# Second and fifth sum of the down weights: where their transfers are issued in a hybrid diffusion layer

## The chip, the core and the metric

The kernel runs on one core of a Trainium2 chip. A core has TensorE (matmul; the profile calls it PE, and its weight loads PEld), VectorE (DVE), ScalarE (ACT), GpSimd (POOL) and SyncE (SP). Each engine works through its own queue in order, and waits at an instruction until the semaphores it names are there. Transfers (DMA) are issued from the queues of SP, POOL and, once, ACT; sixteen DMA engines carry them out. The metric is the time of the slowest core in device microseconds; with one core that is this core's time.

## The reference

One layer on 512 latent tokens of width 1024, with 256 context tokens: a modulated norm, one input projection that feeds a bidirectional Mamba-2 branch and a windowed attention, their merge, and a gated ConvFFN. Cut to what matters here:

```python
p_lat = h_lat @ w_in                                   # z, x/B/C, dt, q, k, v, gates
y_l, _, _ = ssd_bidir(xs_l, bm_l, cm_l, dt_l, la_l, hf_c, hb_c, True)    # the branch
ssd_lat = ssd_output(y_l, xs_l, z, d_skip, ssd_g)
att_lat = window_ctx_attention(q_l, k_l, v_l, k_c, v_c, sink)
x = x + gt1 * ((g_ssd * (ssd_lat @ w_o_ssd) + g_att * (att_lat @ w_o_att)) @ w_out)

def conv_ffn(h, w_up, conv_w, conv_b, w_down):
    u = dwconv_centred(h @ w_up, conv_w, conv_b)       # 2 * 2816 channels
    a, b = u[..., :D_FF], u[..., D_FF:]
    return (jax.nn.silu(a) * b) @ w_down               # the down product, 2816 to 1024

x = rmsnorm(x + gt2 * conv_ffn(modulate(x, norm2_g, sh2, sc2), ...), final_g)
```

The shifts, scales and gates (sh, sc, gt) come from silu(c) @ w_mod.

## The kernel before

Every wide product is made of three passes in a reduced float format: a weight of 128x1024 is loaded by SP (`wraw`, three buffers), ScalarE casts it to a high part (`whi`, L223), VectorE subtracts that to get the low part (`wlo`, L224; L1166 and L1169 in the attention), and TensorE multiplies high by high, high by low and low by high (L295 to L298).

In order of time the program has these stages: the first projections with the modulation (0 to about 60 us), the attention with the q, k, z and output weights beside it (to about 380), the branch (about 430 to 720), the merge and the output projection (to about 860), 22 up steps of the ConvFFN (to 1098), and the down product (to the end).

**The sums of weights.** The down product is made by seven products of half size in place of eight. Four of the operands are sums of the weight's quarters `wdn[0]` to `wdn[3]`, whose signs are folded in by the host. They are computed by transfers alone, in DRAM: a copy of one addend into the sum, then an accumulating transfer of the other. `added` makes the pair; the second waits for the first. With the tile names of the profile: dsum1 = wdn2 + wdn3, dsum4 = wdn0 + wdn2, the second sum dsum2 = dsum4 + wdn3, and the fifth dsum5 = dsum2 + wdn1. Each is cut into four slices of 704 KB, so each sum has four copies and four adds. For eight of the up steps there are sums of the same kind (usum). All of these are issued on POOL's queue by `sum_step` (L182 to L190).

**What sets their order.** `in_turn` mixes the lists of pairs: it keeps three (or four) runs alive and takes one transfer of each in turn. In the attention `product_atoms` (L1143) walks through the weights beside it, numbered g; behind the low part of each, `low` issues the next one to four transfers (L1168), and each waits for that subtraction. The fifth sum goes through the list `LATE`, behind the low parts of the up weights of steps 18 to 21 (`behind`, L232), two for each step.

**The branch** runs over four groups of eight heads. In each, `ssd_steps` goes through four chunks of tokens: POOL scales the states (`st`), makes the diagonals and sums y, VectorE weighs x (`xw`) and adds the states, TensorE multiplies (L1659, L1816, L1824). At the end of a group `gate` (L1857) puts the group's rows to DRAM on SP's queue. Next to the group's end stand the last `ssq` of POOL and, behind it, the first state product of the next group. The next group's projection weights (`wx`), the modulation weights (`wm`, used by VectorE at L868 and L870), decays (`fb`, `far`) and z rows come in on SP's queue around that place.

**The modulation's fold.** A quarter of the modulation is summed over the 128 partitions by nine transfers on POOL's queue, each waiting for the one before: `fold` (L846 to L850), fold6 early in the up steps and fold7 in the late ones. `folded(7)` on VectorE (L854) reads the result before the down product; behind it, in `row_tiles`, a small transpose on TensorE (L2434) stands at the head of the down product.

Of the kernel before, what the change touches and what calls it, by code (L numbers as in the profile page):

```python
# [13 lines left out]
ALU = mybir.AluOpType  # L14
# [10 lines left out]
NFF = 22  # L25
# [14 lines left out]
def raw(ap):  # L40
    return ap.bitcast(F32)
# [3 lines left out]
def tile_hybrid_layer(  # L45
# [33 lines left out]
    V, S, G, T = nc.vector, nc.scalar, nc.gpsimd, nc.tensor  # L79
# [68 lines left out]
            src["dn", DU * j + u] = t[:, 1024 * u : 1024 * u + n], n  # L148

    US = dpool.tile([P, 4, len(SEVEN) * 512], F32, name="usum")  # L150
    SUMS, LATE = [], []

    def added(o, x, y):
        return [(o, x, {}), (o, y, dict(accum_op=ALU.add, max_dma_last_dim=DK * P))]

    def in_turn(runs, n):
        out, live = [], []
        runs = list(runs)
        while runs or live:
            while runs and len(live) < n:  # L160
                live.append(list(runs.pop(0)))
            for r in live:
                out.append(r.pop(0))
            live = [r for r in live if r]
        return out

    RUNS = []
    for q in range(4):
        c = slice(q * DK * P, (q + 1) * DK * P)
        two, four = DSUMS[2][:, c], DSUMS[4][:, c]  # L170
        RUNS.append(added(four, wdn[0][:, c], wdn[2][:, c]) + added(two, four, wdn[3][:, c]))
        RUNS.append(added(DSUMS[1][:, c], wdn[2][:, c], wdn[3][:, c]))
        LATE.append(added(DSUMS[5][:, c], two, wdn[1][:, c]))
    for i in range(0, len(SEVEN), 2):
        c = slice(512 * i, 512 * min(i + 2, len(SEVEN)))
        a0, a1, b0, b1 = (wup7[:, u, c] for u in range(4))
        one, two, three, four = (US[:, u, c] for u in range(4))
        RUNS.append(added(one, b0, b1) + added(two, one, a0) + added(four, two, a1))
        RUNS.append(added(three, a0, b0))
    SUMS, LATE = in_turn(RUNS, 3), in_turn(LATE, 4)  # L180
    BEHIND = mybir.DependencyInfo(mybir.DependencyClass.Sync, mybir.DependencyReason.DATA)

    QUEUED = mybir.DependencyInfo(mybir.DependencyClass.NoSync, mybir.DependencyReason.SCHED_ONLY)
# [1 line left out]
    def sum_step(ins, n=1, SUMS=SUMS):  # L185

        for _ in range(min(n, len(SUMS))):
            o, x, how = SUMS.pop(0)
            dma = G.dma_start(o, x, **how)  # L189
            tc.add_manual_dep(dma.ins, ins.ins.name, BEHIND, reason="weight sums behind a split")  # L190
# [41 lines left out]
    def behind(key):  # L232
        if key[0] == "up":
            SPLITS[key[1]] = F["cast"], F["sub"]
            if key[1] % NFF > 17:
                sum_step(F["sub"], 1, LATE)

    def pinned(t, casts=(), lows=()):
# [246 lines left out]
    with tc.tile_pool(name="spool", bufs=1) as sp:  # L485
# [235 lines left out]
        r = {}  # L721
        cq = tmp("te")[:, :LC]
        for j in range(KT):
# [46 lines left out]
            x = ("hi", "lo") if j >= NU else ("hh", "hl")  # L770
# [31 lines left out]
        for n in range(2):  # L802
            for j in range(KT):
                x = ("hi", "lo") if j >= NU else ("hh", "hl")
# [338 lines left out]
    def product_atoms(g, key, accs):  # L1143

        kind, t = key
        d, R, G_ = {}, 1e6 + 100 * g, "%d" % g
# [19 lines left out]
            S.copy(d["w"][0], d["r"])  # L1166

        def low():  # L1168
            sum_step(V.tensor_tensor(d["w"][1], d["r"], raw(d["w"][0]), ALU.subtract), 1 + (g > 3) + (g > 13) + (g > 21))  # L1169

        def rope_part(f):
            scale = -0.125 if kind == "k" else 1.0
# [37 lines left out]
        rw = R - 2e6 if g != 1 else -500  # L1210
        atom("w" + G_, "ACT", 1.05, was, rw, high, late=g > OLD)
        atom("v" + G_, "DVE", 1.225, ["w" + G_], rw, low, late=g > OLD)
        ks = range(-4 if kind == "k" else 0, 8)
        for k in ks:
# [426 lines left out]
    def ssd_steps(g):  # L1641
        d = GR[g]
# [214 lines left out]
        def gate():  # L1857
            for ct in range(4):
                yz = d["zt"][:, ct, :]
                nc.sync.dma_start(yz_d[4 * g + ct], yz)  # L1860
                SQUARES.append(yz)

        r = [([], states)]
        for c in range(4):
# [895 lines left out]
```

## Time and profile before

| | |
|---|---|
| median of 3 runs | 1213.29 us (1212.75 to 1218.32) |
| profiled execution | 1212.78 us, span of its instructions 1210.8 us |
| TensorE busy | 1198.6 us of the span, 99%, granted clock 0.999 |
| VectorE, ScalarE, GpSimd busy | 946.7, 709.3, 313.3 us |
| transfers | 247.41 MB, 204 GB/s; POOL's queue 44.05 MB, 16.5% of the engines' time |
| sum transfers | 32 on dsum (704 KB), 32 on usum (512 KB) |
| their issue on POOL | dsum from 92.0 us to 1092.6 us, usum from 227.2 to 343.2 us |

How to read it: a busy TensorE includes the modelled ends of its pipelined matmuls, so that a gap of a few tenths of a microsecond can hide. Rows of a timeline give the start, the duration, the engine, the line, output and inputs by name, and in brackets the idle time before with what ended it; "issue" is a wait that the profile does not explain. Issue rows of transfers give the median time from issue to landing; the duration of an issue on POOL is that of making the descriptors, not of the transfer.

### The profile page before, as it was taken

Reading aid. Unit: us, or ns where it says so; the run is one execution under the profiler, and the core shown is the slowest. Engines: PE = TensorE matmul, PEld = TensorE weight load, DVE = VectorE, ACT = ScalarE, POOL = GpSimd, SP = SyncE. Lnnn points to the kernel's source line nnn. Section 1 sums busy time; section 2 is a strip of 40 time slices with the busy share of each in tenths; the row PEclk is TensorE's granted clock in tenths of the full one; section 3 lists DMA queues with packets and bytes.
Section 4 is the critical chain, followed back from the end, with each engine's and each line's share of the span. In section 5 each row is a group of like instructions: output and inputs, shape, how many; then the busy total and the mean of one; then the engine's idle time right before and its main releaser. Section 6 shows DMA issues by size and latency. Waiting matters only on the chain.

```text
span 1210.8 us, 18602 instructions
## 1 busy us (share of the span) xinstructions
PE 1198.6 (99%) x6717; PEld 1014.4 (84%) x6717; DVE 946.7 (78%) x1489; ACT 709.3 (59%) x1311; POOL 313.3 (26%) x314
## 2 busy tenths in 40 slices
PE   9999999999999999999999999999999999999998
PEld 6798888888878878788788778888989998887886
DVE  5857887888666588698887877777699998867787
ACT  5557887787543557486575664223547664345654
POOL 0001112222302647265383681000201211030021
PEclk9999999999999999999999999999999999999999
DMA  9656789998977737566577768677467655579662
GB/s 366 262 144 176 170 232 263 237 210 220 247 192 248 222 116 189 178 152 161 173 173 236 211 203 275 217 255 236 129 163 201 177 179 178 174 204 305 218 186 96
DMA packets 144652, 247.41 MB, mean 204 GB/s; under 512 B 28232, under 2 KB 79728, under 8 KB 144560
## 3 DMA queue, kind: packets, MB, share of 16 engines
q1 hardware_dynamic: 119728, 201.91, 53.8%
q0 software_dynamic: 24544, 44.05, 16.5%
q8 instruction: 53, 0.87, 0.3%
q14 instruction: 39, 0.32, 0.1%
q10 hardware_dynamic: 288, 0.27, 0.1%
HBM read 219.24 MB, written 61.80 MB: 232 GB/s over the span
## 4 chain that ended last, share of the span: by engine, by line
PE 82%; issue 10%; DMA 3%; DVE 2%; POOL 1%; ACT 1%; SPq 0%; DVEq 0%; POOLq 0%; ACTq 0%
PE acc L295 13%; PE acc L298 13%; PE acc L296 13%; PE score L1036 3%; PE po L1085 3%; PE pt L1072 3%; PE mis L639 2%; PE mis L1816 2%; PE mis L1659 2%; DMA xs_d<-xb 2%; PE mis L1824 1%; PE mis L2598 1%; PE acc L2597 1%; PE acc L2598 1%; PE acc L2596 1%
## 5 line engine op out<-in xcount | busy, mean ns | idle before, releaser
L295 PE MATMUL acc<-hlh,whi 128*128 128x512 f32 x472 | 192.8, 409 | 0.0
L298 PE MATMUL acc<-hlh,wlo 128*128 128x512 f32 x472 | 185.5, 393 | 0.0
L296 PE MATMUL acc<-hll,whi 128*128 128x512 f32 x472 | 185.0, 392 | 0.0
L223 ACT CAST whi<-wraw 128x1024 fp32r<-128x1024 f32 (+1 forms) x99 | 103.3, 1044 | 133.1 <-PE acc L296 82.0
L224 DVE TENSOR_TENSOR wlo<-wraw,whi 128x1024 fp32r<-128x1024 f32 (+1 forms) x99 | 129.0, 1304 | 53.6 <-ACT whi L223 52.2
L298 PEld LDWEIGHTS acc<-hlh,wlo 128*128 128x128 f32 x472 | 88.6, 188 | 19.9 <-issue 0.5
L295 PEld LDWEIGHTS acc<-hlh,whi 128*128 128x128 f32 x472 | 88.8, 188 | 17.6 <-issue 2.8
L296 PEld LDWEIGHTS acc<-hll,whi 128*128 128x128 f32 x472 | 88.9, 188 | 17.4 <-issue 2.2
L295 PE MATMUL acc<-mh,whi 128*128 128x512 f32 x240 | 93.5, 390 | 0.0
L296 PE MATMUL acc<-ml,whi 128*128 128x512 f32 x240 | 93.4, 389 | 0.0
L298 PE MATMUL acc<-mh,wlo 128*128 128x512 f32 x240 | 93.4, 389 | 0.0
L1045 DVE CUSTOM_DVE_ANT_0 p<-score,winm,nsink 128x512 f32<-128x512 f32 (+1 forms) x64 | 51.8, 810 | 15.8 <-PE score L1036 14.3
L189 POOL DMA_DIRECT2D dsum<-wdn x24 | 25.1, 1153 | 140.0 <-DVE wlo L1169 82.1
L870 DVE SCALAR_TENSOR_TENSOR tm<-wraw,csil,tm 128x512 f32<-128x512 f32 x56 | 45.7, 816 | 16.7 <-DMA wraw<-wm 16.0
L1052 ACT ACTIVATE p<-p,mneg 128x512 f32<-128x512 f32 (+1 forms) x64 | 49.7, 777 | 15.4 <-DVE mneg L1045 14.8
L1080 DVE TENSOR_TENSOR ptl<-pt,pth 128x512 fp32r<-128x512 f32 x72 | 47.5, 685 | 9.7 <-ACT pth L1076 8.2
L295 PE MATMUL acc<-hch,whi 128*128 128x256 f32 x176 | 53.2, 302 | 0.0
L298 PEld LDWEIGHTS acc<-mh,wlo 128*128 128x128 f32 x240 | 45.1, 188 | 9.4
L295 PEld LDWEIGHTS acc<-mh,whi 128*128 128x128 f32 x240 | 45.1, 188 | 9.3
L296 PEld LDWEIGHTS acc<-ml,whi 128*128 128x128 f32 x240 | 45.1, 188 | 9.1
L1169 DVE TENSOR_TENSOR wlo<-wraw,whi 128x1024 fp32r<-128x1024 f32 x30 | 36.7, 1222 | 18.3 <-ACT whi L1166 18.2
L1781 ACT ACTIVATE E<-fb,TX 128x128 f32<-128x128 f32 x128 | 44.6, 390 | 9.9 <-DMA fb<-cs_d 6.1
(553 smaller groups left out, 3528.6 us busy)
## 6 DMA issues: line engine op xcount, KB each, us to landing
wraw<-wup SPq DMA_DIRECT2D x36, 512.0 KB, 4.1
dsum<-wdn POOLq DMA_DIRECT2D x24, 704.0 KB, 9.4
wraw<-wm SPq DMA_DIRECT2D x32, 512.0 KB, 4.4
fb<-cs_d SPq DMA_DIRECT2D x32, 512.0 KB, 8.1
usum<-wup POOLq DMA_DIRECT2D x24, 512.0 KB, 8.9
wraw<-wx SPq DMA_DIRECT2D x24, 512.0 KB, 3.9
wm<-wm SPq DMA_DIRECT2D x16, 512.0 KB, 8.2
wraw<-wz SPq DMA_DIRECT2D x16, 512.0 KB, 6.7
```

What stands on the lines that cost most here:

```text
L223: F["cast"] = S.copy(hi[:, :n], r[:, :n])
L224: F["sub"] = V.tensor_tensor(lo[:, :n], r[:, :n], raw(hi[:, :n]), ALU.subtract)
L295: T.matmul(ps, wh, xh[:, k0 + k, :], start=a, stop=False)
L296: T.matmul(ps, wh, xl[:, k0 + k, :], start=False, stop=False)
L298: T.matmul(ps, wl, xh[:, k0 + k, :], start=False, stop=b)
L870: V.scalar_tensor_tensor(acc, r[:, u * 512 : u * 512 + 512], sc, acc, ALU.mult, ALU.add)
L1036: T.matmul(ps[:, o : o + len(z) * P], Q[h][:, b * P : (b + 1) * P], k[:, j, z[0] * P : (z[-1] + 1) * P], start=v == 0 and o % 512 in (0, P ...
L1045: V.tensor_tensor_reduce(p[:, :w], d["ps"][i][:, o0 : o0 + w], m, op0=ALU.add, op1=ALU.min, scale=1.0, scalar=nsink[:, h : h + 1], accum_o ...
L1052: S.activation(p, p, AF.Exp, bias=d["mneg"][:, i : i + 1], scale=-1.0, accum_out=d["den"][:, i : i + 1])
L1080: V.tensor_tensor(d["ptl"][x], d["pt"][x], raw(d["pth"][x]), ALU.subtract)
L1169: sum_step(V.tensor_tensor(d["w"][1], d["r"], raw(d["w"][0]), ALU.subtract), 1 + (g > 3) + (g > 13) + (g > 21))
L1781: e0 = S.activation(E[:, u, :], F4[:, u, :], AF.Identity, bias=TX[:, c, 0, h : h + 1])
```

## The change

The transfers that make the second sum (dsum2) leave the list of the attention and go into a list of their own, `MID`: four copies, then four adds. `gate` issues up to three of them behind each group of heads, on POOL's queue, in program order: three copies behind the first group, a copy and two adds behind the second, two adds behind the third. They wait for no subtraction. In the attention the count behind a weight is now one, two from g = 4 and three from g = 20 (before: one, two from 4, three from 14, four from 22), for 48 transfers in place of 56. The fifth sum starts at step 16 in place of 18, so its eight transfers go behind the subtractions of steps 16 to 19.

```diff
-    RUNS = []
+    RUNS, MID = [], []
...
         two, four = DSUMS[2][:, c], DSUMS[4][:, c]
-        RUNS.append(added(four, wdn[0][:, c], wdn[2][:, c]) + added(two, four, wdn[3][:, c]))
+        RUNS.append(added(four, wdn[0][:, c], wdn[2][:, c]))
+        MID.append(added(two, four, wdn[3][:, c]))
...
-    SUMS, LATE = in_turn(RUNS, 3), in_turn(LATE, 4)
+    SUMS, MID, LATE = in_turn(RUNS, 3), in_turn(MID, 4), in_turn(LATE, 4)
...
-            if key[1] % NFF > 17:
+            if key[1] % NFF > 15:
                 sum_step(F["sub"], 1, LATE)
...
-            sum_step(V.tensor_tensor(d["w"][1], d["r"], raw(d["w"][0]), ALU.subtract), 1 + (g > 3) + (g > 13) + (g > 21))
+            sum_step(V.tensor_tensor(d["w"][1], d["r"], raw(d["w"][0]), ALU.subtract), 1 + (g > 3) + (g > 19))
...
                 nc.sync.dma_start(yz_d[4 * g + ct], yz)
                 SQUARES.append(yz)
+            for _ in range(min(3, len(MID))):
+                o, x, how = MID.pop(0)
+                tc.keep_in_program_order(G.dma_start(o, x, **how))
```

The rows of the order below name tiles with their numbers; lines of the changed kernel stand one to four higher than those of the kernel before. PE, DVE, ACT and SP have the same rows in the same order in both.

POOL at the end of the second group of heads (ssq is the last of the group, st the first state product of the next). Before:

```order
L1636 TENSOR_TENSOR zs_5562<-y_5989,zs_5562 128x4x128
L1636 TENSOR_TENSOR y_6150<-te_6132,te_6139 128x512
L1633 TENSOR_TENSOR ssq_115<-ssq_115,sq_6209 128x512
L1636 TENSOR_TENSOR st_6342<-st_6309,eT_3695 128x512
L1636 TENSOR_TENSOR st_6355<-st_6342,eT_3695 128x512
```

Now:

```order
L1637 TENSOR_TENSOR zs_5557<-y_5984,zs_5557 128x4x128
L1637 TENSOR_TENSOR y_6145<-te_6127,te_6134 128x512
L1634 TENSOR_TENSOR ssq_115<-ssq_115,sq_6204 128x512
L1865 DMA dsum2_76<-dsum4_77 128x1408
L1865 DMA dsum2_76<-wdn 128x4x352 x2
L1637 TENSOR_TENSOR st_6340<-st_6307,eT_3687 128x512
L1637 TENSOR_TENSOR st_6353<-st_6340,eT_3687 128x512
```

A copy and two adds now stand between the last ssq of the group and the first state product of the next.

POOL in the late up steps, from the third transfer of the fold on (fold7 is the modulation's fold, mod2 its result). Before:

```order
L848 DMA fold7_767<-fold7_767 128x128
L189 DMA dsum5_78<-dsum2_76 128x1408
L848 DMA fold7_767<-fold7_767 64x128
L848 DMA fold7_767<-fold7_767 32x128
L189 DMA dsum5_78<-dsum2_76 128x1408
L848 DMA fold7_767<-fold7_767 16x128
L848 DMA fold7_767<-fold7_767 16x64
L189 DMA dsum5_78<-dsum2_76 128x1408
L848 DMA fold7_767<-fold7_767 16x32
L850 DMA mod2_95<-fold7_767 128x4x1
L189 DMA dsum5_78<-dsum2_76 128x1408
L189 DMA dsum5_78<-wdn 128x4x352 x4
```

Now:

```order
L190 DMA dsum5_78<-dsum2_76 128x1408
L849 DMA fold7_767<-fold7_767 128x128
L190 DMA dsum5_78<-wdn 128x4x352
L849 DMA fold7_767<-fold7_767 64x128
L849 DMA fold7_767<-fold7_767 32x128
L190 DMA dsum5_78<-wdn 128x4x352
L849 DMA fold7_767<-fold7_767 16x128
L849 DMA fold7_767<-fold7_767 16x64
L190 DMA dsum5_78<-wdn 128x4x352
L849 DMA fold7_767<-fold7_767 16x32
L851 DMA mod2_95<-fold7_767 128x4x1
L190 DMA dsum5_78<-wdn 128x4x352
```

The first three copies of dsum5 have moved ahead of the fold's first transfer (not shown here); where copies stood between its links there are adds now, and one add is left behind its end, where a copy and four adds were.

More of the change, by code (lines that the diff above doesn't have):

```diff
@@ L150, in tile_hybrid_layer @@
     US = dpool.tile([P, 4, len(SEVEN) * 512], F32, name="usum")
-    SUMS, LATE = [], []
+    LATE = []
     def added(o, x, y):
```

## The prediction

> **What bounds the kernel now.** I read the head of the page first, then busy time by stretches, then the places where TensorE is short of its full time.
>
> ```profile
> span 1210.8 us, 18602 instructions
> PE 1198.6 (99%) x6717; PEld 1014.4 (84%) x6717; DVE 946.7 (78%) x1489; ACT 709.3 (59%) x1311; POOL 313.3 (26%) x314
> ```
>
> TensorE is idle for 1210.8 - 1198.6 = 12.2 us. No arithmetic is changed, so only these idle microseconds can be won, and any time is lost only where a transfer or a queue makes TensorE wait. The stretches (start:end in us, length, then busy time and count of PE, PEld, DVE, ACT, POOL, the granted clock, the DMA share, GB/s) say where they lie:
>
> ```profile
> 60.00:380.00 320.00, 318.53 (x1730) 273.06 (x1729) 240.51 (x476) 223.39 (x426) 52.19 (x57) 1.00 0.82 212
> 430.00:660.00 230.00, 229.49 (x1400) 189.41 (x1399) 194.23 (x293) 148.16 (x350) 121.26 (x109) 1.00 0.62 169
> 660.00:720.00 60.00, 58.81 (x328) 46.77 (x327) 48.60 (x69) 37.46 (x86) 42.86 (x38) 1.00 0.69 202
> 1010.00:1100.00 90.00, 90.00 (x399) 74.43 (x399) 72.31 (x102) 39.08 (x52) 17.48 (x18) 1.00 0.67 189
> 1100.00:1115.00 15.00, 13.70 (x60) 10.74 (x59) 11.08 (x15) 8.10 (x10) 0.00 (x0) 1.00 1.06 339
> 1170.00:1211.00 41.00, 34.96 (x163) 29.14 (x161) 34.70 (x51) 22.20 (x35) 5.18 (x7) 0.96 0.42 135
> ```
>
> Idle time of TensorE: 1.47 us in the attention (60 to 380), 0.51 + 1.19 us in the branch (430 to 720), none in the last up steps, 1.30 us at the start of the down product, and 41.00 - 34.96 = 6.0 us (5.8 of them within the span) at the end, which the change does not touch. So at most about 1.47 + 0.51 + 1.19 + 1.30 = 4.5 us is to be won, less than the 0.5% (6.1 us) that a measurement of this kernel can tell from no change.
>
> The 1.30 us at the start of the down product have one cause. First the chain of waits, then TensorE's own rows:
>
> ```profile
> 1099.05 1.24 DVE wlo L224
> 1100.30 8.51 DMA wraw<-wdn
> 1108.84 1.05 ACT whi L223
> 1109.92 1.24 DVE wlo L224
> ...
> 1109.94 0.50 PE L2596 MATMUL mis<-whi,fs 128*128 128x512 f32 x1 [0.77 <-ACT whi L223]
> 1111.20 0.50 PE L2598 MATMUL mis<-wlo,fs 128*128 128x512 f32 x1 [0.53 <-DVE wlo L224]
> ```
>
> A weight load that takes 8.51 us is what the split, and TensorE, wait for. Transfers by issue (out<-in, queue, count, KB, median us to landing), the whole run first, then the three single issues at 1100.3 (weight), 1081.0 (copy) and 1081.6 (add):
>
> ```profile
> dsum<-wdn POOLq DMA_DIRECT2D x24, 704.0 KB, 9.4
> wraw<-wdn SPq DMA_DIRECT2D x11, 512.0 KB, 3.6
> ...
> wraw<-wdn SPq DMA_DIRECT2D x1, 512.0 KB, 8.5
> dsum<-dsum POOLq DMA_DIRECT2D x1, 704.0 KB, 4.4
> dsum<-wdn POOLq DMA_DIRECT2D x1, 704.0 KB, 10.6
> ```
>
> The load needs 3.6 us as a rule and 8.5 us here, where the fifth sum's four adds are in flight: 4.9 us more is the price of adds beside a load.
>
> **The change part by part.** It removes and adds no instruction on TensorE, VectorE or ScalarE; it moves eight transfers (704 KB each, four copies and four adds) from the attention to the branch, and the fifth sum's eight by two up steps.
>
> *Down start.* Rows of GpSimd's queue before it (start, us, what, count, idle time before), with the consumer of the modulation fold on VectorE and on TensorE:
>
> ```profile
> 1057.57 0.81 POOL L189 DMA_DIRECT2D dsum<-dsum  x1
> 1061.25 0.79 POOL L848 DMA_DIRECT2D fold<-fold  x1 [2.87 <-DMA fold<-fold]
> 1080.21 0.84 POOL L850 DMA_DIRECT2D mod<-fold  x1 [3.66 <-DMA fold<-fold]
> 1081.59 3.98 POOL L189 DMA_DIRECT2D dsum<-wdn  x3
> 1092.60 1.25 POOL L189 DMA_DIRECT2D dsum<-wdn  x1 [7.03 <-DVE fs L2123]
> ...
> 1096.41 0.15 DVE L854 TENSOR_TENSOR mod<-mod,vec 128x4 f32<-128x4 f32 x1
> 1098.00 0.27 PE L2434 MATMUL mis<-ident,g2c 128*8 128x128 f32 x1
> ```
>
> Four adds left here from 1081.59 to 1092.60. Now three leave before the fold's end and one behind it, at about 1092, so that only one is still in flight when the load leaves at 1100.30. TensorE reaches its weight at 1109.94 - 0.77 = 1109.2, so the load has 1109.2 - 1100.30 - 1.05 - 1.24 = 6.6 us, against 3.6 us alone. I take the whole 1.30 us as won; the ends are 0 (the remaining add holds it back as before) and -1.3.
>
> *The fold in GpSimd's queue.* The late modulation fold (fold7) is a chain of nine transfers, each of which waits for the one before it. Before, three copies stand between its links; now one copy and three adds do. The queue keeps its order: the link at 1061.25 took 4.3 us behind the copy of 1057.57, the next, with nothing ahead of it, 2.1 us.
>
> ```profile
> fold<-fold POOLq DMA_DIRECT2D x1, 32.0 KB, 4.3
> fold<-fold POOLq DMA_DIRECT2D x1, 16.0 KB, 2.1
> ```
>
> I let a link behind an add land 1.4 us after it, an estimate: two thirds of the 2.1 us that one takes alone. With 9.4 us for an add: first add at 1057.8, its link lands at 1068.6; next link 1071; add at 1069.4 lands 1078.8, links 1080.2 and 1083.2; add at 1081 lands 1090.4, link 1091.8; the last one is issued at 1092 and lands at 1095. VectorE asks for it at 1096.41 (before, it was issued at 1080.21): nothing is lost, by 1.4 us. With the 10.6 us of the crowded add the chain ends three times 1.2 us later, at 1098.6; then VectorE adds, negates, and TensorE transposes at about 1099.2 in place of 1098.00: +1.2 us. I take 0; ends 0 and +1.2.
>
> *The branch.* GpSimd issues three transfers behind the first group of heads, three behind the second, two behind the third. It sits idle there:
>
> ```profile
> 503.50 1.06 POOL L1636 TENSOR_TENSOR st<-st,eT 128x512 f32<-128x512 f32 x1 [14.64 <-ACT st L1680]
> 582.15 1.06 POOL L1636 TENSOR_TENSOR st<-st,eT 128x512 f32<-128x512 f32 x1 [8.30 <-ACT st L1680]
> 660.28 1.06 POOL L1636 TENSOR_TENSOR st<-st,eT 128x512 f32<-128x512 f32 x1 [8.34 <-ACT st L1680]
> ```
>
> At the issue cost in these rows (1.3 us for an add, from 3.98 us for three, and under 0.8 for a copy) three need at most 3.4 of 8.3 us, and every sum that they wait for landed long before, in the attention or a group earlier. Queued behind them is the state product (st), which waits for ScalarE anyway. So the issue costs nothing. The transfers themselves do not: they fly beside the loads of the next group. The one that is used as soon as it lands is the modulation weight, and VectorE stands still for it, with the state weights (xw) for TensorE queued behind. The loads left at 580.5 and 656.4:
>
> ```profile
> wraw<-wm SPq DMA_DIRECT2D x1, 512.0 KB, 4.8
> wraw<-wm SPq DMA_DIRECT2D x1, 512.0 KB, 6.0
> ...
> 588.18 0.75 DVE L1478 SCALAR_TENSOR_TENSOR ta<-acc,half,ta 128x511 f32<-128x511 f32 x1 [0.83 <-ACT ta L1477]
> 589.44 0.68 DVE L1647 TENSOR_TENSOR xw<-xs,TD 128x512 f32<-128x512 f32 x1
> 590.66 1.02 PE L1659 MATMUL mis<-xw,Bk 128*128 128x512 f32 x2
> ...
> 662.39 1.54 DVE L870 SCALAR_TENSOR_TENSOR tm<-wraw,csil,tm 128x512 f32<-128x512 f32 x2 [2.08 <-DMA wraw<-wm]
> 663.85 1.29 DVE L1647 TENSOR_TENSOR xw<-xs,TD 128x512 f32<-128x512 f32 x2
> 665.30 1.02 PE L1659 MATMUL mis<-xw,Bk 128*128 128x512 f32 x2
> ```
>
> Behind the second group VectorE has 0.83 us of idle time and TensorE 590.66 - 590.12 = 0.54 us of slack: lateness beyond 1.4 us is paid. Behind the third the first of two xw ends at about 664.5, so lateness beyond 0.8 us is paid. If each load takes 8.5 us (the row at 1100.3), it is 3.7 and 2.5 us late, and costs 2.3 + 1.7 = 4.0 us. If the adds put their 4.9 us on top of what the loads take now, it is 3.5 + 4.1 = 7.6 us. If the adds have mostly passed by then (they leave from 582.15 - 8.30 = 573.9 and 660.28 - 8.34 = 651.9 on, the loads 4 to 7 us later), it is 0. I take half of the 4.0, +2.0, since adds of 9.4 us end just after the loads would. The three copies behind the first group leave from 503.50 - 14.64 = 488.9 on and have landed by about 500; the state product that follows needs none of them: 0.
>
> The Trainium skill (DMA: Bandwidth & Descriptors, "Anatomy of one DMA — SWDGE (gpsimd) path") fits a transfer from this queue with 2.0 us plus its bytes at 436 GB/s, which makes an estimated 3.7 us for 704 KB; the adds' rows here (9.4 and 10.6 us) say otherwise, and only the copy's 4.4 us comes near. By the page the adds would be gone before either load leaves and the branch would cost 0 in place of +2.0.
>
> *Attention.* Two transfers go beside each weight in the middle where three went, and eight fewer in all. Its 1.47 us of idle time are nearly all one wait:
>
> ```profile
> 208.60 0.36 PE L1036 MATMUL score<-khi,q 128*128 128x256 f32 x1 [1.42 <-DVE wlo L1169]
> ```
>
> Two sum transfers stand beside the weights there before and after, so I take -0.3; ends -1.5 (gone) and 0.
>
> *Up steps.* The adds now fly at 1058 to 1090 beside the up weights, where TensorE has no idle time. A weight's buffer is one of three, and each weight lasts TensorE about 5.4 us, so a load has some 11 us before its split; 4.9 us more is covered: 0.
>
> Sum: -1.3 (down) + 0 (fold) + 2.0 (branch) - 0.3 (attention) + 0 = **+0.4 us** on the profiled execution's 1212.78 us, so 1213.2; the median of the runs shown stands 0.5 us above that execution: **1213.7 us**.
>
> **The rivals.**
> - *The branch hides its transfers.* GpSimd's idle 8.3 us and a DMA share of 0.62 speak for it, the 2.08 us for which VectorE already waits on a modulation weight against it. Then -1.3 - 0.3 = -1.6: 1211.7.
> - *The adds crowd the group boundaries*, the slower side: each modulation load pays the full 4.9 us, VectorE stands, and TensorE pays 7.6 us, less the 1.3 and 0.3: +6.0, so 1219.3. For it speaks the 8.5 us load; against it that at 1100 adds had queued on one another for 18 us, while here only two leave together. It decides from about 0.8 to 1.4 us of lateness of the load.
> - *The fold comes late.* Its slack is only 1.4 us by my sum; +1.2 on top of the forecast: 1214.9. If the adds took 12 us each, it would be three times 2.6 - 1.4 - 1.2 = 5.2 us, but no add alone in its queue does.
> - *The waits in all stages go* (attention, branch and down), the most the idle rows allow: -4.5, 1208.8.
>
> **How the numbers follow.** Forecast 0.50 (1212 to 1216), hidden branch 0.27, crowded boundaries 0.11, late fold 0.08, all waits gone 0.04. Range 1209.5 to 1218.5: it takes in the hidden branch and late fold and leaves out most of the two ends. Faster by over 0.5% is beyond all idle time that can be won, so 0.04; slower by over 0.5% (above 1219.4) is half of the crowded case with a little for a mechanism that I don't see, 0.07; within 0.5%: 0.89.
>
> **What would show it.** Down start: the load that left at 1100.3 lands in under 6.6 us and the stretch 1100 to 1115 has no idle TensorE. Fold: its last transfer is issued between 1085 and 1094, and VectorE has no wait before the add at L854 (L855 after). Branch: longer waits for wraw<-wm behind groups two and three, and gaps of TensorE before L1659 of 0 to 4 us in sum. Wrong would be idle time of GpSimd's issue on the path of st, a TensorE gap in the up steps, or a sum that is not there when the down steps load it.

## The result, and the profile after

The changed kernel takes 1229.01 us (median of 4 runs, 1224.12 to 1229.56) against 1213.02 us of the kernel before beside it (median of 4, 1212.14 to 1218.32). The ratio is 1.0114, with a 95% interval of 1.0075 to 1.0152: **slower by about 1.1%**, where 1213.7 us and no measurable change were forecast. The profiled execution took 1229.16 us.

The head of the page after:

```profile
span 1227.3 us, 18605 instructions
...
PE 1202.4 (98%) x6717; PEld 1016.6 (83%) x6717; DVE 944.5 (77%) x1489; ACT 708.4 (58%) x1311; POOL 313.5 (26%) x314
```

The span is 16.5 us longer. TensorE is idle for 24.9 us in place of 12.2, and busy for 3.8 us more with the same 6717 instructions. The stretches after that answer to those shown of before (the last one, the start of the down product, stands 16.4 us later now):

```profile
60.00:380.00 320.00, 319.94 (x1738) 274.62 (x1737) 239.73 (x475) 224.04 (x427) 46.07 (x51) 1.00 0.74 195
430.00:660.00 230.00, 221.72 (x1360) 183.56 (x1359) 185.65 (x281) 143.34 (x341) 125.36 (x115) 0.99 0.64 176
660.00:720.00 60.00, 55.04 (x280) 42.04 (x279) 43.30 (x62) 31.00 (x73) 32.50 (x30) 0.94 0.82 228
1010.00:1100.00 90.00, 88.58 (x415) 73.71 (x414) 72.47 (x99) 38.50 (x55) 17.08 (x17) 1.00 0.68 201
1116.40:1131.40 15.00, 15.00 (x69) 12.41 (x68) 12.86 (x17) 10.32 (x13) 0.00 (x0) 1.00 0.85 285
```

The attention has won its 1.4 us and the down start its 1.3 us; in the branch (430 to 720) TensorE is busy for 11.5 us less of the same 290 us, and the granted clock is below 1.00.

TensorE runs the same instructions in the same order in both kernels, so the start of one and the same instruction can be compared. How many microseconds later it starts than in the profile of before, at points of the program named by their time in that profile (a row of each later experiment is put here too, so that the reader can come back to it; in e3, e7, e8, e12 and e13 a few neighbouring rows of TensorE are swapped, which moves the figures by tenths at most):

```
start in before      205   215   428   436   500   512   586   594   660   680   708   716   850   862  1000  1060  1105  1115
the change           0.0  -1.7  -2.1  -1.3  -1.3   0.4   0.4   8.8   8.8  16.5  16.5  15.1  15.3  16.3  16.3  18.3  18.3  16.4
e4_held (same)       0.4  -1.2  -1.7  -1.4  -1.4   0.2   0.1   8.9   8.9  14.7  14.7  13.3  13.5  15.7  15.7  15.7  15.7  13.9
e2_branch_alone     -0.3  -2.0  -2.4  -2.1  -2.1  -0.9  -0.9   8.7   8.7  16.7  16.7  15.3  15.6  16.7  16.7  16.7  16.7  14.9
e1_late_alone       -0.3  -0.1  -0.2   0.4   0.4   0.4   0.4   0.4   0.4   0.4   0.4  -1.0  -0.8   0.5   0.5   0.5   0.5  -1.3
e3_first_chunk      -0.2  -1.9  -2.3  -1.9  -1.5  -1.5  -0.4  -0.4   1.5   1.5   1.5   0.1   0.3   1.9   1.9   1.9   1.9   0.0
e5_plain             0.2  -1.5  -1.8  -1.3  -1.3   0.0   0.0   3.5   3.5   8.1   8.1   7.9   8.2  10.1  10.1  10.1  10.1   8.3
e7_held_order        0.0  -1.6  -1.6  -1.3  -1.3  -1.3   0.2   0.2   1.8   6.1   6.3   9.1   8.5   9.1   9.1   9.1   9.1   7.3
e8_held_before       0.0   2.0   2.1   2.5   2.5   2.5   3.9   3.9   5.5   5.5   5.8   6.9   6.6   7.4   7.4   7.4   7.4   5.5
e9_one_by_one       -0.1  -1.7  -2.1  -1.5  -1.5  -1.6   0.1   0.1   1.7   5.5   5.5   8.6   8.0   8.5   8.5   8.5   8.5   6.7
e10_mid_in_up       -0.2  -1.9  -1.9  -1.4  -1.4  -1.4  -1.4  -1.4  -1.4  -1.4  -1.4  -1.1  -1.7  -1.2  -1.1   2.2   2.2   0.4
e11_before_again     0.5   2.6   2.5   3.2   3.2   3.2   3.2   3.2   3.2   3.2   3.2   1.8   2.2   5.4   5.4   5.4   5.4   4.4
e12_away_from_wm    -0.1  -1.8  -2.2  -1.7  -1.2  -1.2  -1.3  -1.3  -1.3  -1.3  -1.3  -1.6  -2.2   2.1   2.1   2.1   2.1   0.3
e13_one_copy_moved  -0.3  -2.0  -2.4  -1.7  -1.1  -1.1  -1.1  -1.1  -1.1  -1.1  -1.1  -1.0  -1.5  -1.3  -1.3  -1.3  -1.3  -2.8
```

The loss is made at three places in the main: behind the first group of heads (500 to 512, +1.7), behind the second (586 to 594, +8.4) and behind the third (660 to 680, +7.7). Smaller losses stand at 850 to 862 (+1.0) and in the up steps at 1000 to 1060 (+2.0); the second of these is missing in the other profile of the same instructions (e4_held). What stands at the three places is VectorE waiting for modulation weights. The waits by pair (who, for whom, total, times, longest), first of before, then of after:

```profile
DVE tm L870 <- DMA wraw<-wm: 16.0, 11, 3.3
```

```profile
DVE tm L871 <- DMA wraw<-wm: 36.7, 11, 9.0
```

The single issues of that load behind groups 1, 2 and 3, of the projection weight just ahead of the second one in SP's queue, and of the transfers that the change puts there (three copies; two adds behind group 2; two adds behind group 3), after:

```profile
wraw<-wm SPq DMA_DIRECT2D x1, 512.0 KB, 6.8
...
wraw<-wm SPq DMA_DIRECT2D x1, 512.0 KB, 13.6
...
wraw<-wm SPq DMA_DIRECT2D x1, 512.0 KB, 11.5
...
wraw<-wx SPq DMA_DIRECT2D x1, 512.0 KB, 12.3
...
dsum<-dsum POOLq DMA_DIRECT2D x3, 704.0 KB, 11.6
...
dsum<-wdn POOLq DMA_DIRECT2D x2, 704.0 KB, 15.6
...
dsum<-wdn POOLq DMA_DIRECT2D x2, 704.0 KB, 15.3
```

The prediction's rows have 4.8 and 6.0 us for the second and third load; they are now 8.8 and 5.5 us longer. The projection weight at 578.2 took 5.7 us before and 12.3 now. Behind group 2 the lateness grows along SP's queue: 6.6 us for this weight, 7.7 for the store issued behind it (`ts_d<-tb`, 4.4 us before, 12.1 now), 8.8 for the modulation weight behind both. All sixteen DMA engines are full there. The queues in the stretch 580 to 592 (packets, MB, share of the sixteen engines' time; q1 is SP's queue, q0 GpSimd's), first of before, where GpSimd's has nothing, then of after:

```profile
q1 hardware_dynamic: 731, 2.10, 49.0%
...
q0 software_dynamic: 945, 1.30, 62.0%
q1 hardware_dynamic: 963, 2.05, 50.3%
```

Together the two queues ask for 112% of the engines' time; the stage's mean of 0.64 (0.62 before) hides this. Whether the full engines alone make the lateness, or the turns between the two queues add to it, was not taken apart. The rows of TensorE behind group 1, and of VectorE and TensorE behind groups 2 and 3, with the idle time ahead of each:

```profile
508.80 1.12 PE L1660 MATMUL mis<-xw,Bk 128*128 128x512 f32 x2 [1.47 <-DVE xw L1648]
```

```profile
594.56 0.75 DVE L871 SCALAR_TENSOR_TENSOR tm<-wraw,csil,tm 128x512 f32<-128x512 f32 x1 [9.05 <-DMA wraw<-wm]
...
677.01 1.54 DVE L871 SCALAR_TENSOR_TENSOR tm<-wraw,csil,tm 128x512 f32<-128x512 f32 x2 [7.91 <-DMA wraw<-wm]
678.47 0.68 DVE L1648 TENSOR_TENSOR xw<-xs,TD 128x512 f32<-128x512 f32 x1
```

```profile
596.06 2.04 PE L1660 MATMUL mis<-xw,Bk 128*128 128x512 f32 x2 [6.77 <-DVE xw L1648]
...
679.21 2.08 PE L1660 MATMUL mis<-xw,Bk 128*128 128x512 f32 x2 [4.96 <-DVE xw L1648]
```

The two products mis<-xw,Bk took 1.02 us before (the prediction's rows at 590.66 and 665.30) and take 2.04 and 2.08 here. The clock that was granted in and behind the gap, in stretches of 3 us (the last three columns are the granted clock, the DMA share and GB/s):

```profile
588.00:591.00 3.00, 1.28 (x8) 0.83 (x6) 0.00 (x0) 0.53 (x1) 0.00 (x0) 1.00 1.09 292
591.00:594.00 3.00, 0.00 (x0) 0.00 (x0) 0.00 (x0) 0.00 (x0) 0.00 (x0) 0.71 1.04 287
594.00:597.00 3.00, 0.94 (x1) 0.50 (x2) 2.44 (x4) 0.00 (x0) 0.00 (x0) 0.50 0.00 0
597.00:600.00 3.00, 3.00 (x14) 2.20 (x12) 2.71 (x6) 0.63 (x1) 1.44 (x1) 0.65 0.50 175
600.00:603.00 3.00, 3.00 (x19) 2.54 (x18) 3.00 (x7) 1.50 (x3) 1.44 (x1) 1.00 0.02 5
```

So a gap of 6.8 us is followed by some 3 us of work at half speed. That makes the cost at group 2 (8.4 us) larger than the gap. Half-speed work behind this gap and the one behind group 3 is what can make up the 3.8 us by which TensorE is "busier".

### The profile page after: what moved, and what is told of

The parts are those of the page before. It is cut to its first block, busy times and chain, and to the rows that moved or that the text cites. A ratio compares the mean times of both kernels' runs of the same rounds, so it can differ in the third digit from the quotient of the medians.

```text
span 1227.3 us, 18605 instructions
## 1 busy us (share of the span) xinstructions
PE 1202.4 (98%) x6717; PEld 1016.6 (83%) x6717; DVE 944.5 (77%) x1489; ACT 708.4 (58%) x1311; POOL 313.5 (26%) x314
## 3 DMA queue, kind: packets, MB, share of 16 engines
q0 software_dynamic: 24544, 44.05, 16.5%
## 4 chain that ended last, share of the span: by engine, by line
PE 76%; issue 11%; DMA 6%; DVE 4%; POOL 1%; ACT 1%; SPq 0%; DVEq 0%; POOLq 0%; ACTq 0%
PE acc L299 12%; PE acc L296 12%; PE acc L297 11%; DMA wraw<-wm 3%; PE score L1037 3%; PE po L1086 3%; PE pt L1073 2%; PE mis L640 2%; PE mis L1817 2%; PE mis L1660 2%; PE mis L2600 2%; PE mis L2602 2%; PE mis L2601 2%; PE mis L1825 1%; PE acc L2600 1%
## 5 line engine op out<-in xcount | busy, mean ns | idle before, releaser
L296 PEld LDWEIGHTS acc<-hlh,whi 128*128 128x128 f32 x472 | 89.1, 189 | 17.8 <-issue 2.9
L190 POOL DMA_DIRECT2D dsum<-wdn x20 | 20.7, 1086 | 128.9 <-DVE wlo L1170 125.9
L1488 ACT ACTIVATE tb<-ta 128x512 f32<-128x512 f32 (+1 forms) x44 | 23.4, 534 | 50.8 <-DVE ta L1482 50.8
```

The source lines that it names most:

```text
L296: T.matmul(ps, wh, xh[:, k0 + k, :], start=a, stop=False)
```

## The experiments

Theory A: transfers of GpSimd's queue beside a group boundary hold back SP's queue; the modulation load at its end is late; VectorE stands for it with xw behind, and TensorE for xw. Rivals: the fifth sum's place carries the loss (D); any such transfers cost that much wherever they stand (B); only the accumulating ones do (C); the projection weights of the same queue would stop TensorE anyway (E).

### The two parts apart

```diff
 e1_late_alone: the change, but
-        RUNS.append(added(four, wdn[0][:, c], wdn[2][:, c]))
-        MID.append(added(two, four, wdn[3][:, c]))
+        RUNS.append(added(four, wdn[0][:, c], wdn[2][:, c]) + added(two, four, wdn[3][:, c]))
...
-            sum_step(V.tensor_tensor(...), 1 + (g > 3) + (g > 19))
+            sum_step(V.tensor_tensor(...), 1 + (g > 3) + (g > 13) + (g > 21))
 e2_branch_alone: the change, but
-            if key[1] % NFF > 15:
+            if key[1] % NFF > 17:
```

> The second sum is back in the attention as before; only the fifth sum stands beside steps 16 to 19. Theory A (the loss of the change is made at the group boundaries of the branch, where the added transfers hold up the modulation weight that VectorE stands for): the branch and the attention are as before; the down start wins about 1.7 us and the up steps lose about 2.0 us, so +0.3 us on 1213.0, ratio 1.000 within 0.002. Rival D (the fifth sum beside steps 16 to 19 carries a good part of the loss): at least +5 us, 1218 or more.

> Only the second sum moves to the gates of the branch; the fifth sum is beside steps 18 to 21 as before. Theory A: attention -1.7, boundaries +1.6, +8.4 and +7.6, -1.4 at the wait near 710 us, +1.0 at the modulation load near 859 us: +15.5 us, so about 1228.5 us, ratio 1.012 to 1.014, with the same three gaps of TensorE before the products mis<-xw,Bk and the 1.3 us stall at the start of the down product as before. Rival D (the fifth sum's place): 1215 or less.

e1_late_alone: 1211.18 us, ratio 0.9993 (0.9980 to 1.0006). e2_branch_alone: 1231.72 us, ratio 1.0154 (1.0132 to 1.0176). The whole loss is in the branch part; D falls. The profiled execution of e2 is the fastest of its five (1227.57 us), so the table shows 4 us less of e2 than its median. The second and third gap stand where they stood:

```profile
595.15 2.05 PE L1660 MATMUL mis<-xw,Bk 128*128 128x512 f32 x2 [7.16 <-DVE xw L1648]
...
678.98 2.07 PE L1660 MATMUL mis<-xw,Bk 128*128 128x512 f32 x2 [4.83 <-DVE xw L1648]
```

Two things went another way than expected. e1 shows no loss in the up steps (0.5 at 862 and at 1105), and e2 has no stall at the start of the down product (16.7 to 14.9), though the fifth sum is in its old place there. Both come back below.

### The same transfers, another place

```diff
 e3_first_chunk: the change, but the loop over MID goes from gate() to the end of chunk_in(c)
+            if not c:
+                for _ in range(min(3, len(MID))):
+                    o, x, how = MID.pop(0)
+                    tc.keep_in_program_order(G.dma_start(o, x, **how))
```

> The change with the same eight transfers of the second sum, three, three and two, on the same queue, but issued in the first chunk of groups 0, 1 and 2 (about 435, 515 and 595 us), where the transfer engines are at 0.2 to 0.4, and not behind the groups. Theory A: the modulation loads at the boundaries take 4 to 6 us again and the gaps before mis<-xw,Bk go; left are attention -1.7, up +2.0, down -1.7: 1210.5 to 1214 us. Rival B (eight such transfers beside the branch cost some 2 us each wherever they stand, by issue on POOL's queue or by bandwidth): 1225 to 1229 us.

1212.49 us, ratio 0.9999 (0.9986 to 1.0012). The three modulation loads at the boundaries take what they took before:

```profile
wraw<-wm SPq DMA_DIRECT2D x1, 512.0 KB, 3.6
...
wraw<-wm SPq DMA_DIRECT2D x1, 512.0 KB, 4.4
...
wraw<-wm SPq DMA_DIRECT2D x1, 512.0 KB, 5.5
```

The same eight transfers in the same branch, at its start (432.6 us) and some 16 us after the loads behind groups 1 and 2 (516.6 and 596.4), cost 3.4 us in place of 17.8 (the table: -1.9 at 436 to 1.5 at 708). B falls: the place makes the price.

### Copies in place of adds

```diff
 e5_plain: the change, but in gate()
-                tc.keep_in_program_order(G.dma_start(o, x, **how))
+                tc.keep_in_program_order(G.dma_start(o, x))
```

> The change with the four accumulating transfers of the second sum behind groups 2 and 3 turned into plain copies of the same 704 KB into the same place (what they should add is left out, so the second sum lacks an addend). Theory A with the bytes as the dose: a copy lands in 4 to 5 us alone where an add takes 9 to 10, so the load behind groups 2 and 3 is late as behind the three copies of group 1 (+3.3 us of load): +1.9 and +1.4 us there in place of +8.4 and +7.6, the whole at 1215 to 1219 us. Rival B (any transfer on POOL's queue halves SP's queue alike): 1227 to 1230 us. Rival C (only accumulating costs anything): the boundaries cost under 0.5 us each, 1211.5 to 1214 us.

1217.91 us, ratio 1.0042 (1.0025 to 1.0060), in the range that theory A gave. The boundaries cost +1.3, +3.5 and +4.6 (the change: +1.7, +8.4, +7.7); the loads behind groups 2 and 3 took 9.6 and 9.1 us:

```profile
wraw<-wm SPq DMA_DIRECT2D x1, 512.0 KB, 9.6
...
wraw<-wm SPq DMA_DIRECT2D x1, 512.0 KB, 9.1
```

So C and "any transfer alike" both fall. A copy holds SP's queue back too, and adds cost 1.7 to 2.4 times as much. My sizes for the single boundaries (+1.9 and +1.4) were too low. GpSimd's queue in the stretch 580 to 592 of e5, to be laid beside the row of the change (945 packets, 1.30 MB, 62.0%):

```profile
q0 software_dynamic: 247, 1.21, 24.1%
```

Nearly the same bytes hold the engines for less than half of the time. The edit takes off two things at once: the accumulation (the addends are left out) and, with the same argument `how`, the cut of each row into four pieces of 352 numbers (128x4x352 in the order rows of the change, 1408 bytes a piece; a copy has 5632). Which of the two makes an add dearer is not shown. The profiled execution of e5 (1220.95 us) is 3 us above its median, so these costs may be high.

### The use put off, the transfers left

```diff
 e4_held: the change, but the first modulation weight of groups 1 to 3 is used one projection later
-        prog += s[0:1] + f + b[0:1] + s[1:2] + s[10:11] + m[0:1] + b[1:2]
+        taken, used = held(m[0]) if m else (None, None)
+        prog += s[0:1] + f + b[0:1] + s[1:2] + s[10:11] + ([taken] if m else []) + b[1:2] + ([used] if m else [])
 e7_held_order: e4_held, and in m_step an order edge behind the newest split for that use
+                if after is not None:
+                    tc.add_manual_dep(x.ins, after, QUEUED, reason="held")
 e8_held_before: the same edge in the kernel before
```

> The change with all transfers where they are; only the use of the first modulation weight of groups 1 to 3 on VectorE is put off until behind the next projection (its load leaves in the same place and holds its buffer longer). Theory A: the load is as late as before (10 to 14 us), but nothing that TensorE needs stands behind it: the gaps of 6.8 and 5.0 us before mis<-xw,Bk fall to under 1.5 us each and the clock stays at 1.00; 1212 to 1217 us. Rival E (the projection weights and z rows in the same queue are late by themselves, so that TensorE stops anyway a few us later): 1221 us or more.

> The run e4_held left VectorE's order as it was (the planner put the use back ahead of xw), so it told nothing. Here an order edge puts the use of the first modulation weight of groups 1 to 3 behind the low part of a later projection weight; all transfers stay where the change has them. Theory A (VectorE standing for the load, with xw behind it, is what TensorE pays): the loads still take 8 to 14 us, but the gaps before mis<-xw,Bk fall under 1.5 us each and the granted clock stays at 1.00; 1213 to 1217 us. Rival E (the projection weights in the same queue are late as well and stop TensorE a few us later): 1221 us or more.

> The control for e7_held_order: the same order edge in the kernel before, with the second sum in the attention. Theory A: VectorE's waits for modulation weights in the branch cost TensorE under 1 us before, so 1211.5 to 1213.5 us. Should the later use hold a weight buffer too long, up to 1218 us, and that much is to be taken off e7_held_order.

e4_held: 1226.57 us, ratio 1.0116 (1.0097 to 1.0135). All engines kept the order of the changed kernel row for row, so this is the changed kernel once more and tells the theories apart in nothing. It is of use as a second profile of it: the +2.0 us that the change's own profile shows in the up steps (16.3 at 1000, 18.3 at 1060) is missing here.

e7_held_order: 1219.06 us, ratio 1.0048 (1.0030 to 1.0067); its control e8_held_before: 1218.32 us, ratio 1.0045 (1.0025 to 1.0064). By the table the boundaries of e7 cost 0.0, 0.0 and +4.3 us, those of e8 nothing, where the change paid 1.7, 8.4 and 7.7. The edge did more than was meant: behind groups 1 and 2 the load of the modulation weight leaves later as well (at 596.6 in place of 580.9), and the next projection weight takes its place in SP's queue. That one is just as late (11.8 us from 580.7 on), and TensorE has no gap there: late projection weights alone cost nothing behind group 2, a late modulation weight with xw behind it cost 8.4 us. That is theory A for group 2. Behind group 3 something is still paid, and not to xw behind a modulation weight. ScalarE's, VectorE's and TensorE's rows:

```profile
671.30 1.05 ACT L224 CAST whi<-wraw 128x1024 fp32r<-128x1024 f32 x1 [5.49 <-DMA wraw<-wg]
```

```profile
672.39 1.23 DVE L225 TENSOR_TENSOR wlo<-wraw,whi 128x1024 fp32r<-128x1024 f32 x1 [6.46 <-ACT whi L224]
```

```profile
675.08 1.70 PE L1662 MATMUL mis<-xw,Bk 128*128 128x512 f32 x2 [2.43 <-DVE xw L1650]
```

A late projection weight (12.8 us from issue to landing) takes the place of the late modulation weight: E holds for group 3, so that my expectation of under 1.5 us was wrong there. The edge itself costs 5 us in the kernel before, in the chunks between the boundaries above all, so that e7 is compared with e8; that their totals are nearly equal rests in part on the attention, where e8, with the second sum still in it, stands at 2.0 at 215 and e7 at -1.6.

### Thinner, or elsewhere

```diff
 e9_one_by_one: e3_first_chunk, but one transfer in the first and one in the second chunk of every group
-            if not c:
-                for _ in range(min(3, len(MID))):
+            if c < 2:
+                for _ in range(min(1, len(MID))):
 e10_mid_in_up: the change without the loop in gate(), and in behind(key)
+            if key[1] < 16:
+                sum_step(F["sub"], 1, MID)
```

> The change with the second sum's eight transfers issued one at a time, in the first and the second chunk of each group, none behind a group; the fifth sum beside steps 16 to 19 as in the change. Theory A: no load at a group boundary is late, no two adds queue on one another; left are attention -1.9 and down -1.3 against the kernel before, and at most +1 in the branch: 1209.5 to 1211.5 us, faster than e3_first_chunk by 1 to 2 us. Rival B (each transfer costs some 2 us anywhere): 1225 us or more. Rival F (the second chunk's loads have no room either): 1213 to 1218 us.

> The change with the second sum's eight transfers in neither the attention nor the branch but in the up steps: one behind the low part of each first half's weight of steps 0 to 4 and 13 to 15; the fifth sum beside steps 16 to 19. Theory A (only loads that VectorE stands for, ahead of work of TensorE, make such transfers dear, and the up steps of e1_late_alone had none): the attention keeps its 1.8 us, the branch is as in the kernel before, the up steps cost under 1 us: 1209.5 to 1212 us, ratio 0.997 to 0.999. Rival B (a transfer costs some 2 us wherever a stage is full): 1222 us or more. Rival G (the early modulation fold in the same queue comes late): a wait of VectorE or TensorE near 860 to 930 us and 1213 to 1217 us.

e9_one_by_one: 1219.48 us, ratio 1.0051 (1.0032 to 1.0069), not as expected: slower than e3 by 7 us, not faster. No modulation load behind a group was late (17.4 us of waits in all, 16.0 in the kernel before). The largest piece (3.8 us from 660 to 680 in the table) has a new wait in the first chunk of group 3, with half-speed work behind it:

```profile
678.35 1.96 PE L1821 MATMUL mis<-CT,st 128*128 128x128 f32 x8 [1.94 <-DVE st L1663]
```

In it an xw on VectorE took 2.32 us at 671.86, beside GpSimd's issue of an add (671.24) and its state product; and a few rows of VectorE's order differ from the changed kernel's. Whether the order or the issue makes that wait was not taken apart. So theory A does not account for every place in the branch that can cost time.

e10_mid_in_up: 1215.44 us, ratio 1.0018 (1.0001 to 1.0036), also above what I expected; its profiled execution (1213.03 us) is 2.4 us below that, so that the rows do not hold all of the loss. Attention and branch are as hoped (-1.4 at 436, -1.1 at 716). The up steps lose 3.3 us between 1000 and 1060, at two places of one kind. VectorE's and TensorE's rows at the first:

```profile
1031.50 0.75 DVE L873 SCALAR_TENSOR_TENSOR tm<-wraw,csil,tm 128x512 f32<-128x512 f32 x1 [3.82 <-DMA wraw<-wm]
```

```profile
1033.44 0.50 PE L301 MATMUL acc<-mh,wlo 128*128 128x512 f32 x1 [1.25 <-DVE wlo L225]
```

A modulation load again, 7.5 us long beside an add, and behind it on VectorE the low part of an up weight. In the change's own profile the +2.0 us of the up steps has the same shape: VectorE waits 3.08 us for `wraw<-wm` at 1062.54, and TensorE 1.20 us for `wlo` at 1067.61.

### The stall of the kernel before

```diff
 e11_before_again: no edit
```

> The kernel before, unchanged, profiled a second time. If the stall of 1.30 us at the start of the down product belongs to the place of the fifth sum, as the prediction had it, the weight load that leaves near 1100 us takes about 8.5 us again and TensorE stands 0.8 and 0.5 us before mis<-whi,fs and mis<-wlo,fs. If it was one execution's chance (the run e2_branch_alone, with the fifth sum in its old place, did not have it), the load takes 4 to 7 us and the stall is gone.

One execution of 1217.24 us. The stall at the down start is there, but less than half of it, and two other gaps are larger than in the first profile: 1.93 us in place of 1.42 at the row of 209.62, and 1.93 in place of 0.26 before mis<-ident,rs at 861.53. The rows of the first and of the down start:

```profile
209.62 0.40 PE L1036 MATMUL score<-khi,q 128*128 128x256 f32 x1 [1.93 <-DMA q<-tc]
...
1115.52 0.50 PE L2598 MATMUL mis<-wlo,fs 128*128 128x512 f32 x1 [0.52 <-DVE wlo L224]
```

With the fifth sum beside steps 18 to 21 the stall was 1.30 and 0.52 us in two profiles (the kernel before) and absent in two others (e2, e8); with it earlier, it was absent in every profile taken. So it was seen with the late place alone, but not in every execution of it.

### Away from the modulation loads

```diff
 e12_away_from_wm: the change without the loop in gate(); in chunk_in(c) of group 0 three copies, and
+            if key[1] < 5:
+                sum_step(F["sub"], 1, MID)
-            if key[1] % NFF > 15:
+            if key[1] % NFF > 16:
 e13_one_copy_moved: e12_away_from_wm, but
-                for _ in range(3):
+                for _ in range(4):
-            if key[1] < 5:
+            if 0 < key[1] < 5:
```

> A version meant to keep the win in the attention and to pay nowhere: three copies of the second sum in the first chunk of the first group of heads, the fourth copy and the four adds behind the low parts of up steps 0 to 4, where e10_mid_in_up lost nothing, and the fifth sum one step later than in the change (steps 17 to 20), behind the last modulation load. Theory A: attention -1.9, branch +0.4, up steps under 0.5, down start 0 to -1.3: 1209.5 to 1212 us, ratio 0.997 to 1.000. Rival B (a transfer costs some 2 us wherever a stage is full): 1222 us or more. Rival G (the adds of steps 1 to 4 hold up the early modulation fold or a load that VectorE stands for): a new wait between 860 and 930 us and 1213 to 1216 us.

> e12_away_from_wm with one copy moved: the fourth copy of the second sum, which there left at 845.4 us beside a modulation load (7.0 us in place of 4.2) ahead of the gap of 3.14 us near 858 us, goes with the other three into the first chunk of the first group; the adds stay behind steps 1 to 4. Theory A: the gap near 858 us falls back to 0.3 to 1.9 us (the kernel before has shown 0.26 and 1.93) with the granted clock at 1.00, the branch's first chunk costs up to 0.5 more; 2 to 3 us less than e12_away_from_wm, 1209.5 to 1211.5 us, ratio 0.997 to 0.9995. If the gap stays at about 3 us, that copy was not its cause, and the time stays at 1212.6.

e12_away_from_wm: 1212.58 us, ratio 1.0007 (0.9994 to 1.0020). The table shows where its win went: from -2.2 at 850 to 2.1 at 862. One copy, the one behind step 0, had left at 845.4 us, 3.4 us ahead of a modulation load. e13 moves that one copy: 1210.27 us, ratio 0.9985 (0.9968 to 1.0002), and the step at 862 is gone (-1.5 to -1.3). Of e12 the load, TensorE's row, and the stretch behind it:

```profile
wraw<-wm SPq DMA_DIRECT2D x1, 512.0 KB, 7.0
```

```profile
858.40 0.69 PE L362 MATMUL mis<-ident,rs 128*128 128x128 f32 x2 [3.14 <-POOL rs L356]
```

```profile
858.00:861.00 3.00, 2.60 (x12) 2.60 (x13) 1.36 (x3) 1.72 (x4) 0.34 (x1) 0.53 0.77 237
```

and the same of e13:

```profile
wraw<-wm SPq DMA_DIRECT2D x1, 512.0 KB, 4.4
```

```profile
856.33 0.43 PE L362 MATMUL mis<-ident,rs 128*128 128x128 f32 x2 [0.38 <-POOL rs L356]
```

```profile
858.00:861.00 3.00, 3.00 (x28) 3.00 (x27) 2.78 (x7) 2.52 (x7) 1.19 (x2) 1.00 0.79 305
```

The step at 862 differs by 4.3 - 0.2 = 4.1 us between these two profiles, and the medians by 2.3 us, with intervals that overlap. That the copy made it is not shown. In e10 the same copy left at 845.1 us, and the load behind it and TensorE's wait were these:

```profile
wraw<-wm SPq DMA_DIRECT2D x1, 512.0 KB, 5.5
```

```profile
856.50 0.43 PE L362 MATMUL mis<-ident,rs 128*128 128x128 f32 x2 [0.82 <-POOL rs L356]
```

With no copy near, this load has taken 4.2 us (the kernel before, wait 0.26), 5.0 (e2, 1.36), 5.7 (e11, 1.93) and 6.1 (e4, 2.48). So TensorE's wait at this place grows with the time of the modulation load, and that time wanders by itself. e13 is the lowest of all versions, but its interval still touches 1: it can't be told from the kernel before.

## Why the prediction was wrong

**What bounds it.** That at most about 4.5 us were to be won was not contradicted: the lowest version stands 1.4 us below the kernel before, which is not told from no change.

**The branch, +2.0 with 7.6 as the upper end: this step failed.** The place, the waiting instruction and what is queued behind it were named right, and theory A of the runs is the "crowded boundaries" rival of the prediction. The size was wrong, at the upper end too: +17.8 us at the three boundaries. With the measured lateness the prediction's own slacks give (8.8 - 1.4) + (5.5 - 0.8) = 12.1 us; with 1.7 us at the first boundary and up to 3.8 us of half-speed work that is 17.6 of the 17.8. Four terms:

- *The length of the adds.* The +2.0 rests on "adds of 9.4 us end just after the loads would". That 9.4 us is the median of 24 rows dsum<-wdn, and eight of them are copies; the sixteen adds alone have 11.0 in the same profile, and of two adds issued together the second took 12.9 to 16.6 us there (issued at 124.9, 164.9, 192.4 and 219.8). In the change the second ones took 18.9 and 18.5 us and landed at 594.5 and 680.0, with the load (594.5) or behind it (677.0).
- *The lateness.* "If the adds put their 4.9 us on top" was meant as the worst case; the loads became 8.8 and 5.5 us later. At the boundaries SP's queue holds gate rows and z rows ahead of the modulation load, behind group 2 a projection weight as well, and these are slowed too (5.7 to 12.3 us for the weight), so that the load comes out later than 4.9 us. The argument against the rival, that only two adds leave together, looked at GpSimd's queue alone, and the DMA share of 0.62 that speaks for the hidden branch is a mean: from 574 to 580 it was 1.04 in the kernel before already.
- *The first boundary, 0.* The three copies were to have landed "by about 500"; they took 11.6 us (median), the last until 502.5, and the load issued at 500.5 took 6.8 in place of 3.5 us. It cost 1.7 us. The term asked only what the state product needs, and left out the load.
- *The clock.* Nothing in the sum stood for half-speed work behind a gap. It made up to 3.8 us of the whole.

The sentence on the Trainium skill (DMA: Bandwidth & Descriptors, "Anatomy of one DMA — SWDGE (gpsimd) path") gave 3.7 us for such a transfer and 0 for the branch; behind groups 2 and 3 the adds took 15.6 and 15.3 us. Its section "Queues, rings and completion order" has each DMA engine take turns between the queues that have work for it; the slower transfers of both queues here agree with that.

**Attention, -0.3: too small.** The wait at 208.60 went, -1.2 to -2.0 us in all ten profiles with the smaller count, while three with the old count show -0.1, 2.0 and 2.6 at the same point. The prediction had -1.5 as an end of this term, and chose against it because two transfers stand beside the weights there before and after. They do, by the issue rows of both profiles, but they are other ones: copies of 704 KB at 200.6 and 206.7 us before, transfers of the up steps' sums of 512 KB at 205.0 and 205.5 now. The count was right, and that it would decide was wrong; that the smaller or later transfers let the q rows land sooner is likely, not shown.

**Up steps, 0: right for the up weights, silent on the modulation's.** The 11 us of lead belong to an up weight. Modulation loads stand between them in the same queue, VectorE waits for those as they land, and a low part waits behind. That cost 2.0 us in one profile of the change and nothing in the other, 3.3 us in e10, and nothing in e1, e3 and e13.

**Down start, -1.3: the size was right, the cause only in part.** The last add landed at 1114.7, before the load that answers to the one of 1100.30 left (1118.6); that load took 5.7 us and TensorE had no gap (the row from 1116.40). But e2 and e8 lack the stall with the fifth sum in its old place, so the 8.51 us row was no fixed price.

**The fold, 0, and GpSimd's issue, 0: right.** GpSimd's rows of the chain's end, and VectorE's use:

```profile
1106.55 0.81 POOL L851 DMA_DIRECT2D mod<-fold  x1 [7.14 <-DMA fold<-fold]
```

```profile
1114.71 0.15 DVE L855 TENSOR_TENSOR mod<-mod,vec 128x4 f32<-128x4 f32 x1
```

The last link left at 1106.55, 1088.2 on the time of before (less the 18.3 of the table), where 1092 was worked out; its use has no wait. Three issues took 3.3 us of GpSimd's idle time behind group 2:

```profile
574.16 0.58 POOL L1865 DMA_DIRECT2D dsum<-dsum  x1
574.75 2.69 POOL L1865 DMA_DIRECT2D dsum<-wdn  x2
```

## What to carry to other kernels

Before a transfer is moved into a stage with idle engines, look not at how busy the transfer engines are there on average (0.62 here, with 1.04 at a boundary), but at which load the program uses the moment it lands, how full the engines are while it flies, what stands ahead of it in its own queue, and what is queued behind the instruction that uses it. A price for "a load beside an add" taken at one place (4.9 us here) is no upper end for another (8.8 and 5.5). Take the length of a transfer from rows of its own kind, issued as many together as the change will issue. And a wait of one or two microseconds that one profile shows should be looked for in a second profile of the same kernel before it is entered in a sum.

## What the runs showed of the hardware that was not expected

**Half clock behind short gaps.** Behind gaps of TensorE of 6.8 and 5.0 us the granted clock stood at 0.50 for 3 to 5 us. It did so behind shorter gaps as well, but not behind all of them: in e5 two gaps before the same product, 2.68 and 2.69 us long, were followed by 1.00 and by 0.50 (the stretches from the end of each):

```profile
591.60:594.60 3.00, 2.64 (x12) 1.77 (x13) 3.00 (x5) 0.00 (x0) 1.16 (x1) 1.00 0.37 135
671.70:674.70 3.00, 3.00 (x6) 1.87 (x7) 2.50 (x6) 0.93 (x4) 0.00 (x0) 0.50 0.99 276
```

In e11 a gap of 1.93 us was enough, in e7 one of 1.55 us (the clock is 0.50 from 720 to 723), while the gaps of 1.42 us in the kernel before, 1.47 us in the change, and 1.55 us at the same product in e8 were not followed by a drop. The Trainium skill (TensorE: Matmul & The Clock Gate, "Part 1: The HAM clock gate") has the clock at half rate after an idle window of about 3.4 us, and full again after as long a busy one, with windows that run on by themselves. The 3 us of half speed agree with that, and so does the dependence on chance; that gaps of 1.55 and 1.93 us suffice does not, and no gap that short could hold a whole window.

**Adds hold the engines longer than copies of the same size.** Behind group 2, 1.30 MB of GpSimd's queue, mostly adds in small pieces, took 62.0% of the sixteen engines' time in 12 us, and 1.21 MB of plain copies 24.1% (e5).

**Scatter of single waits.** e1 is the kernel before up to the late up steps, e11 is the kernel before throughout. Their rows in the table still wander against it, by steps of up to 3.2 us at the same few places (near 209, 710 and 860), to 5.4 us in all. A term of 1 to 2 us read from one trace stands within that.
